# Ten columns of the input projection made for two token blocks from one weight load, in a hybrid decoder layer

## The chip, the cores and the metric

The kernel runs on one core of a Trainium2 chip. The metric is the device time of one execution in microseconds, lower is better. The engines are named as the profile names them: PE is TensorE (matmul) and PEld its loading of a weight matrix into the array, DVE is VectorE, ACT is ScalarE, POOL is GpSimd, SP is the engine whose queue issues the DMA transfers.

## The reference, cut to what matters

One layer of a decoder trunk over 2,048 prompt tokens and 32 sample tokens, width 1,024, in float32. A norm, one input projection to 2,560 columns (20 groups of 128, "columns" below), four mixers that each read a share of them, an output projection, a residual sum, a norm, a squared-ReLU MLP, a last norm:

```python
xn = rmsnorm(h, P['norm1_g'][l])
proj = xn @ P['w_in'][l]
p_ssm, p_q, p_f, p_i, p_g, p_rwkv, p_pool = jnp.split(proj, PROJ_SPLITS, axis=-1)
y_a, s_re, s_im = s5_mixer(p_ssm, ...)      # columns 0 and 1
y_b, s_hg = hgrn2_mixer(p_q, p_f, p_i, p_g, ...)   # columns 2 to 9
y_c, s_wkv, s_sh = rwkv7_mixer(p_rwkv, ...)  # columns 10 to 17
y_d, s_pool = pool_mixer(p_pool, ...)        # columns 18 and 19
mixed = jnp.concatenate([y_a, y_b, y_c, y_d], axis=-1).astype(h.dtype)
h = h + mixed @ P['w_out'][l]
h = h + sqrelu_mlp(rmsnorm(h, P['norm2_g'][l]), P['mlp_up'][l], P['mlp_down'][l])
```

The mixers are recurrent: each block of tokens needs the state that the block before it left.

## The kernel before, in words

The tokens lie along the free axis, in six blocks of 256, 384, 384, 384, 384 and 288 tokens (block 0 to block 5); features lie on the 128 partitions. Each matrix product is made in three matmuls on rounded parts: `mm24` runs 8 chunks of the contraction with three matmuls each (lines 157 to 159), 24 for one column of one block, each with its own load of 128 x 128 weights into the array.

A column's weights come as one transfer of 512 KB (`wload`, tile `raw`, two buffers), are rounded by ScalarE (`whi`, line 128) and subtracted by VectorE (`wlo`, line 129), three buffers each. `next_w` keeps one column split ahead, in the order of the list `wseq`, which `init_weights` writes: the columns of block 0 in order `IORD0`, those of block 1 in order `IORD1`, then output projection, MLP and later columns.

`inproj(b, part)` makes the columns of one block; `evac` takes a finished column out of PSUM (one of four tiles `mm`). Block 0 is not yet normalised there: its scale `y1` is multiplied in by VectorE in `evac`. Block 1 is normalised beforehand by `norm1(1)`: eight loads of x (line 204, two small buffers `xs`), the sum of squares (`sumsq`, lines 188 to 192), the scale (`rstd`, lines 168 to 178), then eight reloads of x, eight multiplications (line 216) and splits (lines 198 and 199) into `AB`, the operand of block 1's columns. Columns 0 to 9 of block 1 go to the tile `P10` (region `act1`), columns 10 to 17 to `P8` (region `h1`), columns 18 and 19 to the tile `pu`, which all blocks share. At the start `h1` holds block 0's x and then the scratch tile `su` of the SSM setup.

Beside the columns run generators that each yield after a step: `ssm_setup` (17 steps: constants of the SSM, mostly GpSimd, written to DRAM at the end), `lane1` (RWKV; 37 steps for block 0's two pairs of 128 tokens with their groupnorms), `lane2` (HGRN; 13 steps for each of block 0's two pairs), `l3` (SSM, 16 steps; needs the setup), and `lane4` (pooling, which reads `pu` and uses scratch that the setup leaves). `weave` advances each by a rate per step of the main generator; `drive` advances an interleaving of lanes 1, 2 and 3 by three steps per column. Then what is left of block 0's lanes is run out, with the next block's lanes taking turns as soon as one ends, and block 0's output projection begins; it reads all four mixers' results.

The order of this emission sets priorities: the framework's planner orders each engine's queue by it, and puts an instruction that it thinks ready ahead of earlier ones that are not. On the chip each engine then keeps the planned order. Tiles of one name reuse their buffers when the last reader is done.

Of the kernel before, what the change touches and what calls it, by code (L numbers as in the profile page):

```python
# [21 lines left out]
PM = 4  # L22
QA = lambda f: False
IORD = list(range(10)) + [18, 19] + list(range(10, 18))
IORD1 = list(range(20))
IORD0 = list(range(10, 18)) + list(range(2, 10)) + [18, 19, 0, 1]
CUT = 11
LAG = 2
HK = ()
# [1 line left out]
OK0 = (6, 7, 2, 3, 0, 1, 4, 5)  # L31
DEF = (0, 5)
WARM = 24
S1 = (1, 1, 0, 1, 8)
R1 = 3
S0 = (.6, 1, .06, 1, 3, 3, 3, .25, 1)
NG = {4: 1, 5: 1, 6: 9}


# [9 lines left out]
BLK = blocks()  # L49
# [3 lines left out]
class Main:  # L53
# [32 lines left out]
    def init_weights(self):  # L86
# [7 lines left out]
        outp = list(range(20, 28))  # L94
        seq += IORD0 + IORD1
        for b in range(nb):
# [125 lines left out]
    def scaled_parts(self, src, n, gcol, dst, square, ks=range(8)):  # L222

        nc = self.nc
        acc = None
        for k in ks:
            s = src(k)
            g = self.pp[:, gcol + k:gcol + k + 1]
            nc.scalar.activation(out=dst[:, k, :n], in_=s, func=AF.Copy, scale=g)
            nc.vector.scalar_tensor_tensor(out=dst[:, 8 + k, :n], in0=s, scalar=g, in1=dst[:, k, :n], op0=ALU.mult, op1=ALU.subtract)  # L230
            if square:
                acc = self.sumsq(lambda k: s, n, (k,), acc)
        return acc

    def norm1(self, b):
        return self.norm_to(lambda k: self.xload(b, k), BLK[b][2], 0, self.X(b))
# [143 lines left out]
def weave(main, *others, steps=None):  # L380

    acc = [0.0] * len(others)
    i = 0
    while i != steps:
        if next(main, END) is END:
            return
        i += 1
        for j, (g, rate) in enumerate(others):
            acc[j] += rate
            while acc[j] >= 1:  # L390
                acc[j] -= 1
                next(g, None)
# [64 lines left out]
def program(m):  # L457
    nb = len(BLK)
    if WARM:
        m.warm()  # L460
    run = lambda g: [None for _ in g]
    m.norm1_first()
    m.first_regions()
    m.l3 = m.lane3(0)
    main, setup, l1, l2, n1 = m.inproj(0, IORD0), m.ssm_setup(), m.lane1(0), m.lane2(0, False), m.norm1(1)
    weave(main, (setup, S0[0]), steps=8)
    weave(main, (l1, S0[1]), (setup, S0[2]), (n1, S0[7]), steps=8)
    weave(main, (l1, S0[1]), (setup, S0[2]), (l2, S0[3]), (n1, S0[8]))
    weave(n1, (l1, S0[4]), (setup, S0[5]), (l2, S0[6]))
    main = m.inproj(1, IORD1)  # L470
    weave(main, (l1, S1[0]), (l2, S1[1]), steps=S1[2])
    weave(main, (l1, S1[0]), (l2, S1[1]), (setup, S1[3]), steps=S1[4] - S1[2])
    run(setup)
    run(m.lane4())
    ready, done = [], []
    side = interleave(then(l1, done, ready, m.lane1(1)), then(l2, done, ready, m.lane2(1)), then(m.l3, done))
    drive(main, side, R1, rest=False)
    ready.append(1)
    while len(done) < 3:
        next(side)  # L480
    for b in range(nb):
        last = b + 1 == nb
        fin = m.final(b - 1) if last else None
        if last:
            next(fin)
        m.alloc_mlp(b)
        if last:
            run(lag_(m.outproj(b), fin, LAG))
            run(m.norm2(b))
        elif b:  # L490
            run(m.outproj(b))
            run(lag(m.inproj(b + 1, IORD[CUT:]), m.norm2(b), LAG))
        else:
            run(m.outproj(b))
            run(m.norm2(b))
        if b:
            side = None if last else m.mixers(b + 1)
        main = [m.mlp(b, m.norm1(b + 2) if b + 2 < nb else None)]
        if b + 2 < nb:
            main.append(lag(m.inproj(b + 2, IORD[:CUT], True), m.final(b), LAG * (2 if HK else 1)))  # L500
        elif last:
            main.append(m.final(b))
        drive(chain(*main), side, RATIO if b else R0)
        if b + 2 == nb:
            m.states_out()
# [101 lines left out]
class Mix(Main):  # L607
# [139 lines left out]
        nc.scalar.copy(self.sh[:, 1, i, :], v(ps[:, np_:n])[:, :, 3])  # L747

    def iord(self, b):
        return (IORD0, IORD1)[b] if b < 2 else IORD  # L750

    def region(self, b, k, tag, name):
        t = self.big.tile([128, k, NMAX], F32, tag=tag, name=name)
# [2 lines left out]
    def inproj(self, b, part, steps=False):  # L756
        n = BLK[b][2]
        X = self.X(b)
        held = []
        for c in part:  # L760
            if b and c == next(x for x in self.iord(b) if x < 10):
                self.P10[b % 2] = self.region(b, 10, f"act{b % 2}", "P10")
            if b and c == next(x for x in self.iord(b) if 10 <= x < 18):
                self.P8[b % 2] = self.region(b, 8, f"h{b % 2}", "P8")
            w = self.next_w(c)
            ps = self.psum()
            for _ in self.mmg(ps, w, lambda k: (X[:, k, :n], X[:, 8 + k, :n]), n):
                if steps:
                    yield
            held.append((c, ps))  # L770
            if b == 0 and c == part[0]:
                continue
            if b == 0 and c == part[1]:
                self.y1 = self.rstd(self.acc0, n)
            while held:
                self.evac(b, *held.pop(0))
            yield


    def rwkv_prep(self, b, c0, pool, par):  # L780
# [1256 lines left out]
```

## Time and profile before

| | |
|---|---|
| median of three runs | 2715.27 us (2713.78 to 2718.02) |
| the profiled execution's own time | 2714.48 us |
| its span, first to last instruction | 2712.6 us |
| TensorE busy / weight loads into the array | 97% / 92% |
| VectorE / ScalarE / GpSimd busy | 72% / 53% / 13% |
| mean granted TensorE clock | 0.982 of full speed |
| moved by DMA | 366.28 MB, 135 GB/s |

Busy shares are means over the span; a matmul's end is modelled, so a busy TensorE is not one at its peak. A granted clock of 1.00 is 2.4 GHz, 0.50 is 1.2 GHz; values between are means over a stretch that has both.

### The profile page before, as it was taken

What the parts mean: (1) busy time and instruction counts of PE and PEld (TensorE: products, weight loads), DVE (VectorE), ACT (ScalarE), POOL (GpSimd) and SP (SyncE); (2) the same over time, 40 slices, a digit from 0 to 9 for tenths busy, and PEclk for the clock granted to TensorE, in tenths of its full rate; (3) what the DMA queues carried; (4) which work ended last, traced back from release to release, by engine and by line L of the source; (5) the groups of instructions that cost most, each with busy time, mean ns of one, the idle gap of its engine ahead of it and who ended that gap; (6) DMA issues with size and microseconds to landing.
All of it is one profiled execution on the core that took longest, in us unless ns stands there. A gap on an engine that the chain in (4) does not pass through costs nothing.

```text
span 2712.6 us, 52883 instructions
## 1 busy us (share of the span) xinstructions
PE 2629.4 (97%) x20466; PEld 2492.0 (92%) x20466; DVE 1955.7 (72%) x4324; ACT 1438.6 (53%) x2377; POOL 357.5 (13%) x864
## 2 busy tenths in 40 slices
PE   8799899899999999999999999999999999999998
PEld 8688799889999999999999999999999989899997
DVE  7886888874877777487777748777775786557666
ACT  6544766544656545375654536565454754445443
POOL 7631201100111100001110010111001100000000
PEclk9799999999999999999999999999999999999999
DMA  6543344564333255532335553223555334435553
GB/s 208 142 126 98 124 148 134 156 190 147 115 96 98 96 166 165 166 119 88 99 101 174 167 160 113 94 91 107 173 177 159 100 103 122 133 115 169 167 168 127
DMA packets 221068, 366.28 MB, mean 135 GB/s; under 512 B 105520, under 2 KB 140912, under 8 KB 220816
## 3 DMA queue, kind: packets, MB, share of 16 engines
q1 hardware_dynamic: 220816, 362.90, 43.1%
q8 instruction: 161, 2.64, 0.4%
q14 instruction: 91, 0.75, 0.1%
HBM read 343.26 MB, written 17.99 MB: 133 GB/s over the span
## 4 chain that ended last, share of the span: by engine, by line
PE 74%; DVE 11%; DMA 5%; ACT 4%; POOL 3%; issue 2%; SPq 1%; DVEq 0%; ACTq 0%; POOLq 0%
PE mm L157 21%; PE mm L158 21%; PE mm L159 21%; DVE wlo L129 3%; DMA raw<-w 2%; PE x L1272 1%; ACT whi L128 1%; POOL XD L887 1%; POOL tm L885 1%; DMA xs<-xT 1%; PE x L687 1%; PE x L1828 1%; PE x L1827 1%; DMA mt<-dB 1%; PE x L951 1%
## 5 line engine op out<-in xcount | busy, mean ns | idle before, releaser
L128 ACT CAST whi<-raw 128x1024 fp32r<-128x1024 f32 x552 | 577.5, 1046 | 773.0 <-PE mm L158 528.0
L157 PE MATMUL mm<-AB,whi 128*128 128x384 f32 (+2 forms) x2880 | 950.4, 331 | 14.2 <-ACT whi L128 5.2
L159 PE MATMUL mm<-AB,wlo 128*128 128x384 f32 (+2 forms) x2880 | 936.2, 325 | 4.2 <-DVE wlo L129 3.8
L158 PE MATMUL mm<-AB,whi 128*128 128x384 f32 (+2 forms) x2880 | 935.2, 325 | 1.0 <-DVE AB L199 0.8
L129 DVE TENSOR_TENSOR wlo<-raw,whi 128x1024 fp32r<-128x1024 f32 x552 | 678.4, 1230 | 274.2 <-ACT whi L128 271.6
L157 PEld LDWEIGHTS mm<-AB,whi 128*128 128x128 f32 x2880 | 545.9, 190 | 27.3 <-ACT whi L128 6.3
L159 PEld LDWEIGHTS mm<-AB,wlo 128*128 128x128 f32 x2880 | 547.1, 190 | 9.3 <-DVE wlo L129 6.3
L158 PEld LDWEIGHTS mm<-AB,whi 128*128 128x128 f32 x2880 | 547.6, 190 | 6.7 <-DVE AB L199 1.4
L157 PE MATMUL mm<-act,whi 128*128 128x384 f32 (+2 forms) x1536 | 497.7, 329 | 4.6 <-ACT whi L128 2.5
L158 PE MATMUL mm<-act,whi 128*128 128x384 f32 (+2 forms) x1536 | 493.9, 323 | 0.5 <-DVE act L329 0.3
L159 PE MATMUL mm<-act,wlo 128*128 128x384 f32 (+2 forms) x1536 | 492.2, 322 | 0.0
L157 PEld LDWEIGHTS mm<-act,whi 128*128 128x128 f32 x1536 | 289.6, 190 | 12.9 <-DVE h L338 2.8
L158 PEld LDWEIGHTS mm<-act,whi 128*128 128x128 f32 x1536 | 291.2, 190 | 5.5 <-issue 2.3
L159 PEld LDWEIGHTS mm<-act,wlo 128*128 128x128 f32 x1536 | 290.6, 190 | 1.6 <-issue 0.2
L338 DVE TENSOR_TENSOR h<-h,mm 128x384 f32<-128x384 f32 (+2 forms) x384 | 192.5, 510 | 96.4 <-PE mm L159 95.6
L885 POOL TENSOR_TENSOR tm<-sq,XD 32x15 f32<-32x15 f32 (+7 forms) x240 | 90.7, 378 | 563.0 <-DMA sq<-XC 545.6
L329 DVE TENSOR_TENSOR act<-q,act 128x384 fp32r<-128x384 f32 (+2 forms) x192 | 98.9, 516 | 6.2 <-ACT q L326 1.7
L324 ACT ACTIVATE act<-r 128x384 fp32r<-128x384 f32 (+2 forms) x192 | 94.2, 490 | 13.3 <-DVE r L323 11.0
L887 POOL TENSOR_TENSOR XD<-XD,tm 32x15 f32<-32x15 f32 (+7 forms) x240 | 85.4, 356 | 18.5
L880 POOL MEMSET XD<- 32x512 f32 x16 | 8.3, 516 | 578.2 <-PE x L969 346.1
L192 DVE TENSOR_TENSOR acc<-acc,sq 128x384 f32<-128x384 f32 (+2 forms) x126 | 64.8, 514 | 15.7 <-ACT sq L191 13.3
L328 DVE TENSOR_TENSOR q<-r 128x384 f32<-128x384 f32 x128 | 71.1, 555 | 0.6 <-ACT r L321 0.5
(584 smaller groups left out, 3110.4 us busy)
## 6 DMA issues: line engine op xcount, KB each, us to landing
raw<-w SPq DMA_DIRECT2D x552, 512.0 KB
xs<-xT SPq DMA_DIRECT2D x96, 192.0 KB
yT<-xo SPq DMA_DIRECT2D x32, 192.0 KB
mt<-dB SPq DMA_DIRECT2D x20, 256.0 KB
mt<-dT SPq DMA_DIRECT2D x20, 256.0 KB
mt<-dC SPq DMA_DIRECT2D x20, 256.0 KB
xs<-xT SPq DMA_DIRECT2D x24, 144.0 KB
rt<-dRot SPq DMA_DIRECT2D x16, 98.0 KB
```

The costliest lines, as they stand in the source:

```text
L128: nc.scalar.copy(hi, raw)
L129: (nc.gpsimd if GW(i) else nc.vector).tensor_tensor(out=lo, in0=raw, in1=hi, op=ALU.subtract)
L157: nc.tensor.matmul(ps[:, :n], a, xh, start=k == ks[0], stop=False)
L158: nc.tensor.matmul(ps[:, :n], a, xl, start=False, stop=False)
L159: nc.tensor.matmul(ps[:, :n], c, xh, start=False, stop=k == ks[-1])
L192: nc.vector.tensor_tensor(out=acc[:, :n], in0=acc[:, :n], in1=q[:, :n], op=ALU.add)
L324: nc.scalar.activation(out=self.act[:, s, 0, :n], in_=r[:, :n], func=AF.Square)
L328: nc.vector.tensor_tensor(out=q[:, :n], in0=r[:, :n], in1=r[:, :n], op=ALU.mult)
L329: nc.vector.tensor_tensor(out=self.act[:, s, 1, :n], in0=q[:, :n], in1=self.act[:, s, 0, :n], op=ALU.subtract)
L338: nc.vector.tensor_tensor(out=self.h[:, d, :n], in0=self.h[:, d, :n], in1=ps[:, :n], op=ALU.add)
L885: g.tensor_tensor(out=w, in0=U[:, 0:t, t:t + 1].to_broadcast([32, t, m]), in1=XT[:, t:t + 1, t:16].to_broadcast([32, t, m]), op=ALU.mult)
L887: g.tensor_tensor(out=XT[:, 0:t, t:16], in0=XT[:, 0:t, t:16], in1=w, op=ALU.add)
```

## The change

Block 0 first makes its RWKV and pooling columns alone (10 to 19). Beside them block 1's norm is made by the new `norm1_second`: x is loaded once, into the region `act1`, and kept there for both passes. Then ten columns (2 to 9, 0 and 1) are made for both blocks, each from one transfer and one split of its weights (`inproj_both`). Then block 1 makes its own remaining ten, the pooling columns first. The rates at which the lanes and the setup advance are new: RWKV begins with the both-block columns (one step per block's column, 20 in all), HGRN with the last two of them (4 steps), and the setup makes 5 steps under the first ten columns, some 3 under the next ten, and the rest is emitted after them, followed by `lane4`. The stage with three lanes has 10 columns instead of 12.

```diff
-IORD1 = list(range(20))
-IORD0 = list(range(10, 18)) + list(range(2, 10)) + [18, 19, 0, 1]
+RWT = list(range(10, 18))
+BOTH = list(range(2, 10)) + [0, 1]
+IORD0 = RWT + [18, 19]
+IORD1 = BOTH + [18, 19] + RWT
...
-S1 = (1, 1, 0, 1, 8)
+S0 = (.5, 1.8)
+S1 = (1, .2, 1)
 R1 = 3
-S0 = (.6, 1, .06, 1, 3, 3, 3, .25, 1)
...
+    def norm1_second(self):
+
+        n = BLK[1][2]
+        x = self.region(1, 10, "act1", "x1")
+        acc = None
+        for k in range(8):
+            self.nc.sync.dma_start(out=x[:, k, :n], in_=self.D["xT"][128 * k:128 * k + 128, BLK[1][0]:BLK[1][0] + n])
+            acc = self.sumsq(lambda k: x[:, k, :n], n, (k,), acc)
+            yield
+        yield from self.norm_to(lambda k: x[:, k, :n], n, 0, self.X(1), acc)
...
-    main, setup, l1, l2, n1 = m.inproj(0, IORD0), m.ssm_setup(), m.lane1(0), m.lane2(0, False), m.norm1(1)
-    weave(main, (setup, S0[0]), steps=8)
-    weave(main, (l1, S0[1]), (setup, S0[2]), (n1, S0[7]), steps=8)
-    weave(main, (l1, S0[1]), (setup, S0[2]), (l2, S0[3]), (n1, S0[8]))
-    weave(n1, (l1, S0[4]), (setup, S0[5]), (l2, S0[6]))
-    main = m.inproj(1, IORD1)
-    weave(main, (l1, S1[0]), (l2, S1[1]), steps=S1[2])
-    weave(main, (l1, S1[0]), (l2, S1[1]), (setup, S1[3]), steps=S1[4] - S1[2])
+    main, setup, l1, l2, n1 = m.inproj(0, IORD0), m.ssm_setup(), m.lane1(0), m.lane2(0, False), m.norm1_second()
+    weave(main, (setup, S0[0]), steps=2)
+    weave(main, (setup, S0[0]), (n1, S0[1]))
+    run(n1)
+    main = m.inproj_both(BOTH)
+    weave(main, (l1, S1[0]), (setup, S1[1]), steps=16)
+    weave(main, (l1, S1[0]), (l2, S1[2]), (setup, S1[1]))
     run(setup)
     run(m.lane4())
     ready, done = [], []
+    main = m.inproj(1, [18, 19] + RWT)
...
+    def inproj_both(self, part):
+
+        for c in part:
+            w = self.next_w(c)
+            if c == part[0]:
+                self.P10[1] = self.region(1, 10, "act1", "P10")
+            for b in range(2):
+                X, n = self.X(b), BLK[b][2]
+                ps = self.psum()
+                self.mm24(ps, w, lambda k: (X[:, k, :n], X[:, 8 + k, :n]), n)
+                self.evac(b, c, ps)
+                yield
```

## Rows read from the trace of the kernel before

**Rows 1.** Windows, from 300 us to the end; columns as in rows 3.
```profile
300.00:2712.60 2412.60, 2366.58 (x18291) 2251.28 (x18291) 1726.62 (x3768) 1273.92 (x2092) 223.69 (x534) 0.99 0.43 134
```

**Rows 2.** Timeline of PE at 79 us; bracketed: idle before, releaser.
```profile
79.10 0.47 PE L1272 MATMUL x<-P,E 64*64 64x64 f32 x2 [8.51 <-ACT E L1209]
```

**Rows 3.** Windows: stretch, length, busy PE, PEld, DVE, ACT, POOL, PEclk, DMA, GB/s.
```profile
8.40:49.20 40.80, 34.46 (x247) 32.29 (x245) 27.96 (x64) 23.66 (x38) 30.46 (x92) 0.92 0.64 198
96.80:110.40 13.60, 6.21 (x60) 4.72 (x58) 13.56 (x34) 6.26 (x12) 5.20 (x8) 0.65 0.88 221
110.40:129.10 18.70, 17.91 (x88) 15.69 (x87) 17.52 (x39) 8.67 (x19) 11.67 (x26) 0.71 0.50 134
129.10:187.50 58.40, 55.75 (x527) 50.55 (x526) 46.14 (x111) 32.16 (x54) 25.53 (x51) 0.94 0.43 116
187.50:255.20 67.70, 66.14 (x643) 62.31 (x642) 45.65 (x143) 25.24 (x43) 11.76 (x35) 0.97 0.44 126
255.20:281.00 25.80, 20.03 (x133) 17.13 (x133) 18.45 (x41) 19.49 (x36) 9.02 (x14) 0.88 0.08 27
```

**Rows 4.** Timelines of PE and DVE: the norm of block 1.
```profile
69.68 0.81 PE L168 MATMUL nrm<-acc,ones 128*128 128x384 f32 x2
...
105.78 0.54 DVE L178 TENSOR_TENSOR ny<-ny,nt 128x384 f32<-128x384 f32 x1
...
126.47 1.08 DVE L199 TENSOR_TENSOR AB<-xn,AB 128x384 fp32r<-128x384 f32 x1
```

**Rows 5.** Timeline of PE (start us, length us): matmuls 18, 18, 12 apart.
```profile
94.10 0.28 PE L157 MATMUL mm<-AB,whi 128*128 128x256 f32 x1
96.23 0.28 PE L157 MATMUL mm<-AB,whi 128*128 128x256 f32 x1
...
229.53 0.34 PE L157 MATMUL mm<-AB,whi 128*128 128x384 f32 x1
232.69 0.34 PE L157 MATMUL mm<-AB,whi 128*128 128x384 f32 x1
...
79.89 0.41 PE L157 MATMUL mm<-AB,whi 128*128 128x256 f32 x1
82.45 0.41 PE L157 MATMUL mm<-AB,whi 128*128 128x256 f32 x1
```

**Rows 6.** Lines, first 260 us (count | busy us, mean ns | idle before).
```profile
L129 DVE TENSOR_TENSOR wlo<-raw,whi 128x1024 fp32r<-128x1024 f32 x43 | 53.9, 1255 | 21.0 <-ACT whi L128 20.8
L216 DVE SCALAR_TENSOR_TENSOR xn<-xs,pp_sb,ny 128x384 f32<-128x384 f32 x8 | 6.9, 878 | 0.8 <-DMA xs<-xT 0.7
L199 DVE TENSOR_TENSOR AB<-xn,AB 128x384 fp32r<-128x384 f32 x8 | 4.9, 631 | 0.1
L192 DVE TENSOR_TENSOR acc<-acc,sq 128x384 f32<-128x384 f32 x7 | 3.9, 550 | 1.1 <-ACT sq L191 1.1
```

**Rows 7.** Timelines of PE and SP: the setup's closing matmuls, last transfers.
```profile
151.58 0.57 PE L1727 MATMUL mm<-su 128*16 128x128 f32 x2
...
181.48 3.65 SPq L1731 DMA_DIRECT2D dT<-su  x8
```

**Rows 8.** Lines, 160 to 266 us: HGRN operations of the second pair.
```profile
L1287 DVE COPY_PREDICATED P<-cst,x 128x32 f32<-128x32 int32 x24 | 2.7, 195 | 0.0
L1413 ACT ACT_TABLE_LOAD x2 | 2.6, 1283 | 2.2 <-DVE E L1412 2.2
L1272 PE MATMUL x<-QK 64*64 64x32 f32 x96 | 2.5, 220 | 0.0
L1415 DVE TENSOR_TENSOR eb<-eb,E 128x256 f32<-128x256 f32 x2 | 0.9, 426 | 2.8 <-ACT E L1414 2.8
```

**Rows 9.** Timeline of all engines: the tail.
```profile
256.11 0.68 PE L987 MATMUL x<-sv,M 128*64 128x64 f32 x8
...
277.32 0.42 DVE L1185 TENSOR_TENSOR AB<-Y,AB 128x256 fp32r<-128x256 f32 x1
...
281.91 0.36 PE L157 MATMUL mm<-AB,whi 128*128 128x256 f32 x1
```

More of the change, by code (lines that the diff above doesn't have):

```diff
@@ L749, in iord @@
     def iord(self, b):
-        return (IORD0, IORD1)[b] if b < 2 else IORD
+        return IORD1 if b < 2 else IORD
     def region(self, b, k, tag, name):
```

## The prediction

> **What bounds the kernel now.** I cut the span into stages with the table of windows, at the ends of columns as the timeline of TensorE shows them. From 300 us on TensorE is busy 2366.6 of 2412.6 us at a granted clock of 0.99 [rows 1]: there is little left to win there, nothing after it is edited, and whatever is won or lost before 300 us is carried to the end almost unchanged. Only time in which TensorE stands still or runs slowly counts. So the whole question lies in the first 281 us: 20 columns for the first block (to 96.8 us), 20 for the second (110.4 to 255.2), with the first block's mixers in between, and a tail to 281 in which the output projection waits for the last mixer results.
>
> In the first 281 us the reader is to see three losses. At 70.6 us TensorE stops for 8.51 us in the middle of a column, because a matmul of the HGRN lane stands ahead of the column's others in its queue and waits for ScalarE [rows 2]. From 96.8 to 110.4 no column runs; VectorE is busy 13.56 of 13.60 us there [rows 3]. The reason is the second block's norm: its sum of squares left TensorE at 69.68 us, the scale was ready at 106.3 and the last normalised part at 127.6 [rows 4], each step standing in VectorE's full queue. Then the first two columns of the second block take 18.7 us, part of it at half clock (0.71 in that window).
>
> What a column costs when nothing waits: 18 of its 24 matmuls are 2.13 us apart at 256 tokens, so 2.85 for 24; 3.16 us at 384 tokens, so 4.21; and at half clock 12 take 2.56 us, so 5.1 a column of 256 tokens [rows 5].
>
> **The change, part by part.** It removes ten loads of 512 KB, ten ScalarE casts and ten VectorE subtractions of 1.26 us [rows 6]. It does not remove one matmul or one array weight load: each block still runs 24 of each per column. So on TensorE it saves nothing directly; the ten subtractions are 12.6 us of an engine that is full only in the two stages from 96.8 to 129.1 (31.1 of 32.3 us) [rows 3]. What counts is the new order, and I add it up as a clock, stage by stage.
>
> *Stage 1, ten columns of block 0 with the norm beside them.* Before, the tenth column ends at 49.2 us, and VectorE worked 27.96 of the 40.8 us [rows 3]. The norm adds 3.9 + 6.9 + 4.9 us [rows 6] and five short operations of about 0.5 [rows 4], near 18 us: 46 us of work, over 40.8. It cannot be hidden wholly. Its eight loads of x (192 KB) are no longer held back by two small buffers, and eight reloads vanish, since x stays in the free `act1` region; but the loads go out in SP's queue among the first weights, while DMA already works at 0.64 [rows 3]. If VectorE were always busy the norm would be done at 54.4, at 90% at 59.5. The columns need only their own small evacuations, so I take 52 for the tenth column (49.2 to 57), and 4 us (0 to 10, the latter being 18.7 minus two columns in today's wait) lost before the second block's columns run freely: 56.
>
> *Stage 2, ten columns for both blocks.* 10 x (2.85 + 4.21) = 70.6 us, with 20 steps of the RWKV lane, 4 of HGRN and some 4 of the SSM setup between them. Today's 187.5 to 255.2 holds ten columns (42.1) and 30 lane steps, so 25.6 us or 0.85 a step; 129.1 to 187.5 holds eight columns (33.7) and 24 steps, so 1.03 a step [rows 3]. 28 steps are 24 to 29; I take 24, since VectorE has its load halved here (one subtraction per 7 us). The stage ends at 56 + 70.6 + 24 = 150.6. Today the same thirty column pieces are done at 187.5.
>
> *Handover.* Here the new order costs. Columns 18 and 19 of block 1 come first in the next stage, but their target `pu` is still being read by block 0's pooling, which waits for the rest of the setup (now all emitted after the both-block columns); and the RWKV columns write the region `h1`, which the setup holds until its last copies to DRAM. Today the setup's last transfers go out at 181.5 to 185.1, after its first closing matmuls at 151.6 [rows 7]; the pooling is done earlier, and nothing waits, since the first RWKV column of block 1 starts only at 187.5. In the new order that is 33.5 us counted from 150.6, so to 184. Four PSUM tiles let four columns go ahead of their evacuation, 4 x (4.21 + 2.56, the lane steps of a column) = 27 us: 6.5 left, or 13 if one of the four is in use by the setup or the SSM lane, or nothing if the planner draws the setup's work forward. I take 5.
>
> *Stage 3, ten columns of block 1 with 30 lane steps:* today's 67.7 us for the same count [rows 3]. End: 150.6 + 5 + 67.7 = 223.3, against 255.2 today.
>
> *The tail.* HGRN has 26 steps for block 0. Today 14 are emitted before the three-lane stage and 12 in it: none is left when the columns end, only 3 of RWKV. In the new order HGRN starts 4 steps before that stage and makes 10 in it; 12 steps, nearly all of its second pair, are left with no column to hide them, beside 7 of RWKV and 4 of SSM. The pair's own durations one after another, from the table of lines [rows 8]: the masks 2.7, the level matmuls 2.5 and as many again for their other part and the state, two table loads 2.6, and some 45 further operations, most near 0.43 and some below 0.3, about 18: 28 us, the lower bound. It does not have its engines alone: in today's tail VectorE is busy 18.45 and ScalarE 19.49 of 25.8 us [rows 3], largely for the other lanes. With its engines two thirds of the time the chain takes 42, which I take (28 to 74, the latter below): 265.3.
>
> *After it* three output columns, of which only the pooling quarter can be done in advance: 3 x 2.85 x 0.75 = 6.4, partly at half clock: 7. The fourth would start at 272.3; today it starts at 281.9 [rows 9]. That is 9.6 us sooner. The profiled execution took 2714.48 us (span 2712.6), 0.8 below the median of the runs: 2714.5 - 9.6 + 0.8 = 2705.7.
>
> On that tail the rows say that after stretches with few matmuls the granted clock is low (0.65 and 0.71 in the two windows after 96.8, 0.88 in today's tail) [rows 3]. The Trainium skill, "TensorE: Matmul & The Clock Gate", Part 1, states the rule behind it: the throttled clock is the default and activity releases it. By the rule the longer tail would leave all three output columns at half clock, 3 x 5.1 x 0.75 = 11.5 instead of 7, and the sum would be 2710; by today's tail, where only some of their matmuls are slow, it is 2706. The same page (Part 2) says that matmuls stay in program order, which is what the 8.51 us wait shows and what can happen anew wherever a lane's matmul is placed too early.
>
> **The rivals.**
> *The tail eats more than was won (slower).* Place: from the last column of block 1 to the last write of HGRN's second pair. Today's tail runs the last 3.5 RWKV steps from 256.11 to 277.74, 21.6 us [rows 9], 6.2 a step; twelve at that rate are 74 us, 32 more than I took: +22, 2738 us. It decides from a tail of 51.6 us (4.3 a step) on. For it: three lanes interleave there, each engine takes them in the planner's order, and the clock is low. Against it: groupnorm's steps, which fill today's tail, are longer than most of HGRN's.
> *The handover and the norm eat it (same).* The upper bound of 13 instead of 5 and 2 us more in stage 1: 2716, within 0.2% of before (5.4 us, about what a measurement can tell from no change). For it: two regions and the PSUM tiles are shared. Against: the setup's VectorE and GpSimd work is ready early, and GpSimd is busy only 25.5 of the 58.4 us from 129.1 on [rows 3].
> *The tail is hidden (faster still).* If the pair runs at its own durations, 28: 14 us less, 2692. For it: VectorE is busy only 45.65 of today's 67.7 us of stage 3 [rows 3], so the pair's first steps could run ahead. Against: in today's tail each step takes far longer than its own operations.
> *That the change does nothing* is excluded: 542 weight casts in place of 552, and the order differs from the first microseconds on.
>
> **How the numbers follow.** My forecast, 2698 to 2709, has 0.45; the hidden tail 0.12; the handover case 0.20; the long tail 0.23. Faster by over 0.2%: 0.57; within: 0.20; slower: 0.23. The range runs from just under the hidden tail, 2690, into the long one, 2728 (that is, a tail of 64 us).
>
> **What would show it.** Right: 542 casts; no column-free stretch like 96.8 to 110.4; the second block's norm done by about 60 us; the thirtieth column piece at about 151, the last column of block 1 at about 223, the fourth output column at about 272, and an unchanged course after it. Wrong: in stage 1, if the tenth column ends after 57; at the handover, if columns stand for more than 13 us behind `pu` or `h1`; in the tail, if it lasts over 51 us; or if the time after 300 us changes by more than 2 us, which no term here explains.

## The result, and the profile after

The changed kernel takes 2749.33 us (2747.84 to 2752.75, 4 runs) beside 2714.53 for the kernel before on the same chip: ratio 1.0115, 95% interval 1.0102 to 1.0129. It is slower by 35 us; 2706 was forecast, with a range up to 2728. The profiled span is 2746.7 us against 2712.6. One of the executions of run e1 below is left out of its numbers: it took 3173.92 us at a granted clock of 0.743.

The same stages as in [rows 3], cut at the ends of columns. Windows of the changed kernel: stretch, length, busy PE, PEld, DVE, ACT, POOL, PEclk, DMA share, GB/s:

```profile
8.05:60.11 52.06, 37.69 (x257) 34.27 (x256) 34.81 (x78) 32.72 (x54) 38.38 (x118) 0.90 0.63 199
60.11:103.92 43.81, 34.12 (x223) 33.32 (x222) 32.45 (x60) 17.97 (x35) 28.44 (x70) 0.88 0.24 70
103.92:160.90 56.98, 54.78 (x457) 51.41 (x455) 33.71 (x76) 24.56 (x44) 18.88 (x41) 1.00 0.31 88
160.90:188.49 27.59, 12.96 (x98) 8.74 (x97) 23.01 (x48) 10.88 (x20) 17.93 (x41) 0.70 0.41 101
188.49:251.63 63.14, 63.14 (x581) 59.25 (x582) 37.86 (x124) 26.16 (x42) 11.44 (x33) 0.97 0.43 127
251.63:304.33 52.70, 37.63 (x392) 31.98 (x393) 36.51 (x118) 28.54 (x56) 8.34 (x16) 0.71 0.12 25
345.19:358.73 13.54, 5.00 (x76) 3.97 (x76) 11.83 (x36) 7.62 (x16) 0.00 (x0) 0.63 0.29 95
622.00:2746.00 2124.00, 2093.41 (x15544) 1993.81 (x15544) 1489.42 (x3184) 1099.54 (x1788) 183.42 (x429) 1.00 0.42 133
```

The reader is to see two stretches in which TensorE does little at a low granted clock while VectorE is busy: 160.90 to 188.49, where no column runs (VectorE 23.0 of 27.6 us), and 345.19 to 358.73 (11.8 of 13.5). In a table, against the clock that the prediction set up:

| point | forecast | measured | before |
|---|---|---|---|
| tenth column of block 0 ends | 52 | 60.1 | 49.2 |
| thirtieth column piece ends | 150.6 | 160.9 | 185.5 |
| time without columns after it | 5 | 27.6 | 2.1 |
| last column of block 1 ends | 223.3 | 251.6 | 255.2 |
| last mixer result written | 265.3 | 294.6 | 277.3 |
| fourth output column starts | 272.3 | 304.3 | 281.9 |

Up to there the forecast is 32.0 us out: 10.3 in the first two stages, 22.6 in the handover, 4.6 back in stage 3, 1.0 in the tail (43.0 for 42) and 2.7 in the output columns. Behind that point "an unchanged course" was forecast. It did not come. The offset of a column below is its start minus that of the same column in the kernel before, columns counted from the last one backwards: +22.4 us at the fourth output column, +24.3 at the first up column (before: 301.1 us), +39.3 at the first down column (324.2), +31.6 at 622 us and at 666, +33.9 at the last column.

Block 1's norm, forecast for about 60, has its scale at 61.3 us and its last part at 87.4. The largest wait of stage 1 stands before its tenth column: a lane's matmul waits for ScalarE, then the norm's first matmul for VectorE, and the column comes behind both. Timeline of PE (start us, length us; bracketed: idle before, releaser):

```profile
50.95 0.37 PE L825 MATMUL x<-tha,wl 64*128 64x128 f32 x1 [1.37 <-ACT tha L819]
...
54.06 1.65 PE L170 MATMUL nrm<-acc,ones 128*128 128x384 f32 x2 [2.39 <-DVE acc L194]
54.94 0.99 PE L159 MATMUL mm<-AB,whi 128*128 128x256 f32 x1
```

The handover, timeline of PE:

```profile
174.69 3.59 PE L1753 MATMUL mm<-su 128*16 128x128 f32 x16
187.53 1.03 PE L1753 MATMUL mm<-su 128*16 128x128 f32 x4 [9.25 <-DVE su L1743]
188.49 0.69 PE L159 MATMUL mm<-AB,whi 128*128 128x384 f32 x1
```

The setup's first group of closing matmuls (line 1727 of the kernel before) and four of the second come first and the columns behind them; the second group waits for VectorE's line 1743. After 345 us it is the scale of block 0's second norm that is late (lines 174 to 180; line 336 is the first evacuation of an up column, which needs it). Timeline of DVE, only some of the operations in between:

```profile
337.38 0.42 DVE L174 TENSOR_SCALAR acc<-nrm 128x256 f32<-128x256 f32 x1
343.56 0.43 DVE L177 TENSOR_TENSOR nt<-ny 128x256 f32<-128x256 f32 x1 [2.02 <-ACT ny L176]
...
345.29 0.42 DVE L1232 SCALAR_TENSOR_TENSOR lf<-P,L 128x256 f32<-128x256 f32 x1 [0.97 <-ACT L L1230]
...
347.66 0.42 DVE L178 TENSOR_TENSOR nt<-nt,acc 128x256 f32<-128x256 f32 x1
...
349.58 0.29 DVE L179 TENSOR_SCALAR nt<-nt 128x256 f32<-128x256 f32 x1
349.79 1.22 DVE L131 TENSOR_TENSOR wlo<-raw,whi 128x1024 fp32r<-128x1024 f32 x1
350.92 1.10 DVE L1270 TENSOR_TENSOR QK<-bb 128x128 f32<-128x128 f32 x5
...
353.71 0.42 DVE L180 TENSOR_TENSOR ny<-ny,nt 128x256 f32<-128x256 f32 x1
...
357.52 0.43 DVE L336 SCALAR_TENSOR_TENSOR r<-mm,ny 128x256 f32<-128x256 f32 x1
```

Five operations that need 2 us on VectorE take 16.7 from first to last. The way over ScalarE behind the first of them takes 5.8 us, hardly more than in the kernel before (5.3); the last four take 10.6 where there it is 1.7, since block 1's HGRN (lines 1232 and 1270) and weight splits stand between them. Four up columns fill the four PSUM tiles meanwhile; the fifth starts at 358.73, 1.2 us after the first evacuation began. In the kernel before the same chain has nothing between its last four steps and ends in 7.4 us:

```profile
313.25 0.42 DVE L172 TENSOR_SCALAR acc<-nrm 128x256 f32<-128x256 f32 x1 [1.59 <-PE nrm L168]
318.98 0.42 DVE L175 TENSOR_TENSOR nt<-ny 128x256 f32<-128x256 f32 x1 [2.02 <-ACT ny L174]
...
320.22 0.45 DVE L178 TENSOR_TENSOR ny<-ny,nt 128x256 f32<-128x256 f32 x1
```

### The profile page after: what moved, and what is told of

It is laid out like the page before. It is cut to its first block, busy times and chain, and to the rows that moved or that the text cites. A ratio compares the mean times of both kernels' runs of the same rounds, so it can differ in the third digit from the quotient of the medians.

```text
span 2746.7 us, 52803 instructions
## 1 busy us (share of the span) xinstructions
PE 2633.7 (96%) x20466; PEld 2494.7 (91%) x20466; DVE 1947.0 (71%) x4314; ACT 1433.2 (52%) x2369; POOL 356.9 (13%) x864
## 4 chain that ended last, share of the span: by engine, by line
PE 70%; DVE 10%; POOL 5%; DMA 5%; ACT 4%; issue 3%; SPq 2%; DVEq 0%; ACTq 0%; POOLq 0%
PE mm L159 20%; PE mm L161 20%; PE mm L160 20%; DVE wlo L131 2%; DMA raw<-w 2%; POOL XD L913 2%; POOL tm L911 2%; PE x L1298 1%; ACT whi L130 1%; PE x L700 1%; PE x L1853 1%; PE x L1854 1%; DMA xs<-xT 1%; DMA yT<-xo 1%; PE x L995 1%
## 5 line engine op out<-in xcount | busy, mean ns | idle before, releaser
L130 ACT CAST whi<-raw 128x1024 fp32r<-128x1024 f32 x542 | 566.5, 1046 | 772.0 <-PE mm L160 551.0
L131 DVE TENSOR_TENSOR wlo<-raw,whi 128x1024 fp32r<-128x1024 f32 x542 | 665.4, 1228 | 279.3 <-ACT whi L130 270.9
L911 POOL TENSOR_TENSOR tm<-sq,XD 32x15 f32<-32x15 f32 (+7 forms) x240 | 98.6, 411 | 532.5 <-DMA sq<-XC 515.4
L194 DVE TENSOR_TENSOR acc<-acc,sq 128x384 f32<-128x384 f32 (+2 forms) x126 | 65.9, 523 | 11.8 <-ACT sq L193 9.2
```

The source lines that it names most:

```text
L130: nc.scalar.copy(hi, raw)
L131: (nc.gpsimd if GW(i) else nc.vector).tensor_tensor(out=lo, in0=raw, in1=hi, op=ALU.subtract)
L194: nc.vector.tensor_tensor(out=acc[:, :n], in0=acc[:, :n], in1=q[:, :n], op=ALU.add)
L911: g.tensor_tensor(out=w, in0=U[:, 0:t, t:t + 1].to_broadcast([32, t, m]), in1=XT[:, t:t + 1, t:16].to_broadcast([32, t, m]), op=ALU.mult)
```

## The experiments

All results in one table; the text takes them in turn. "u" is the offset of the first up column, "d" that of the first down column, "m" that at 666 us, the second block's last output column. Offsets come from one profiled execution each. In the thirteen other runs whose first stage is emitted as in the change the tenth column ends at 57.1 to 59.5 us (60.1 in the change), so differences of up to 3 us between offsets say little.

| run | us | ratio to before | u | d | m |
|---|---|---|---|---|---|
| the change | 2749.3 | 1.0115 (1.0102 to 1.0129) | +24.3 | +39.3 | +31.6 |
| e1 setup early | 2743.0 | 1.0092 (1.0071 to 1.0114) | +16.6 | +28.8 | +22.6 |
| e2 setup's PSUM | 2749.6 | 1.0110 (1.0094 to 1.0125) | +22.9 | +37.6 | +30.7 |
| e3 lanes held | 2743.9 | 1.0091 (1.0074 to 1.0107) | +22.1 | +30.3 | +27.7 |
| e4 norm only | 2741.9 | 1.0079 (1.0063 to 1.0096) | +20.0 | +25.8 | +22.3 |
| e5 norm, steps kept | 2722.8 | 1.0021 (1.0012 to 1.0030) | +3.1 | +3.9 | +0.8 |
| e6 HGRN ahead | 2744.5 | 1.0103 (1.0082 to 1.0125) | +25.5 | +32.1 | +26.9 |
| e7 setup and lanes | 2728.0 | 1.0035 (1.0016 to 1.0055) | +3.5 | +9.8 | +9.5 |
| e8 lanes held, 5 | 2768.6 | 1.0185 (1.0168 to 1.0202) | +23.0 | +31.9 | +49.6 |
| e9 e7, lanes held | 2732.6 | 1.0054 (1.0038 to 1.0070) | +3.1 | +10.0 | +18.5 |
| e10 two loads | 2746.6 | 1.0110 (1.0089 to 1.0131) | +28.1 | +37.8 | +28.7 |
| e11 lanes held, 17 | 2786.1 | 1.0251 (1.0228 to 1.0275) | +20.8 | +29.0 | +66.7 |
| e12 no norm | 2738.8 | 1.0082 (1.0062 to 1.0102) | +17.0 | +31.5 | +19.8 |
| e13 no second scale | 2741.0 | 1.0089 (1.0072 to 1.0106) | +24.2 | +19.8 | +20.9 |
| e14 e7, no second scale | 2721.0 | 1.0021 (1.0011 to 1.0032) | -0.3 | -2.1 | -0.4 |
| e15 scale on GpSimd | 2743.2 | 1.0090 (1.0076 to 1.0104) | +23.9 | +29.7 | +26.3 |
| e16 e7, scale on GpSimd | 2730.6 | 1.0043 (1.0029 to 1.0057) | +2.6 | +4.6 | +12.8 |
| e17 before, setup ops moved | 2715.6 | 0.9990 (0.9980 to 0.9999) | -2.5 | -2.3 | 0.0 |
| e18 e7, setup ops moved | 2725.4 | 1.0025 (1.0014 to 1.0036) | -3.7 | +3.5 | +5.2 |

**e1, the setup earlier.** The setup's rate beside the both-block columns, and two steps of the SSM lane that it carries put behind those columns:

```diff
-S1 = (1, .2, 1)
+S1 = (1, .65, 1)
-    run(setup)
+    next(m.l3), next(m.l3), run(setup)
```

> The changed kernel with the SSM setup emitted faster beside the both-block columns (rate .65 in place of .2), so that its closing steps no longer stand between those columns and the second block's own. Theory (the closing steps, emitted last, hold the columns): the 27.6 us without columns shrink to under 6, and the time falls by 17 to 22 us to 2727-2732. Rival (the closing steps cost their engine time wherever they are): the both-block columns, 101 us long, grow by about what the gap loses, and the time stays within 5 us of 2749.

Windows from the last both-block column on:

```profile
169.56:171.69 2.13, 2.13 (x19) 1.72 (x19) 1.83 (x4) 1.51 (x4) 0.00 (x0) 1.00 0.27 40
171.69:237.11 65.42, 65.42 (x638) 60.80 (x638) 41.80 (x135) 28.05 (x47) 12.13 (x35) 1.00 0.44 127
237.11:299.65 62.54, 42.45 (x399) 36.11 (x399) 42.61 (x131) 34.06 (x65) 9.77 (x16) 0.67 0.13 30
```

The 27.6 us shrink to 2.1: late setup steps do stop the columns. The price is another matter. The both-block stage ends 8.7 us later (169.6), the last column 14.5 us sooner, and the stretch from it to the fourth output column is 62.5 us instead of 52.7: of 25.5 us taken out, 4.7 are left at that column. Both theories were partly right, neither in its number.

**e2, the setup's PSUM tiles.** Both kinds of closing matmuls:

```diff
-                pt = self.psum().rearrange("p (a n) -> p a n", a=4)
+                pt = self.px().rearrange("p (a n) -> p a n", a=4)
-                pg = self.psum()
+                pg = self.px()
```

> The changed kernel, but the setup's transposes and closing matmuls write the lanes' PSUM tiles and not the four of the columns. If the four PSUM tiles are what holds the second block's own columns behind the setup, the pooling columns 18 and 19 run ahead of the setup's last matmuls: 8 us (two columns of 4.2) come off the gap of 27.6, and 2741 is to be seen. If the regions pu and h1, or VectorE and GpSimd, hold them, the gap stays above 25 us and the time within 3 us of 2749.

Columns 18 and 19 now do run ahead (161.9 to 173.7), and then the stop is back, 27.73 us; the last column ends 2.5 us sooner, and nothing is left of it in the time. Columns put into the gap bring nothing: they were not what the first block's end waits for.

**e3, block 1's lanes held** until block 0's have ended:

```diff
-    ready.append(1)
     while len(done) < 3:
         next(side)
+    ready.append(1)
```

> The changed kernel, but the second block's lanes may not begin before all three of the first block's have ended. After the tail the changed kernel lost another 12 us beside the up columns. Theory (the second block's lane matmuls, emitted during the long tail, stand in TensorE's queue ahead of the up columns and wait): the stop of 13.5 us at 345 us goes, 2737-2740. Rival (the second norm's own chain is late behind the crowded VectorE and ScalarE): the first down column stays 36-39 us later than in the kernel before, and the time stays within 4 us of 2749 or rises, since lane work is lost from the tail.

The stop before the fifth up column falls from 13.5 to 9.4 us only, the chain of the scale to 15.5. Neither forecast hit; e8, e11, e13 and e15 go on with it.

**e4 and e5, the norm alone** in the kernel before, at 1.8 steps a column from the third on; e5 (last two lines) also keeps what the norm's last step carried:

```diff
-    main, setup, l1, l2, n1 = m.inproj(0, IORD0), ..., m.norm1(1)
+    main, setup, l1, l2, n1 = m.inproj(0, IORD0), ..., m.norm1_second()
...
-    weave(n1, (l1, S0[4]), (setup, S0[5]), (l2, S0[6]))
+    weave(iter([0]), (l1, S0[4]), (setup, S0[5]), (l2, S0[6]))
```

> The kernel before with one part of the change alone: the second block's norm made beside the first block's columns from x kept in the act1 region; no shared columns, no other order. If that norm was what made the 13.6 us without columns and the two slow columns after them (18.7 us for two, 8.4 when nothing waits), 10 to 20 us come off: 2695-2705. Rival (VectorE is the limit there and the norm's 18 us only move): the first twenty columns end later by what the stretch loses, and the time stays within 5 us of 2714.

> The norm alone once more, in the kernel before, but with the three steps each of RWKV, setup and HGRN put back that were carried by the norm's last step and were lost in the run before this one. Theory (the lost steps made that run slow: the setup's closing steps then stopped the columns for 17 us): that stop falls below 6 us and the kernel comes out 5 to 15 us under the kernel before, 2700-2710. Rival (the norm beside the first block's columns is itself the loss): it stays over 2730.

e4 lost 22 us, with a stop of 17.0 us at 162.6 us; three steps more of RWKV, of HGRN and of the setup take it away (3.3 us at that place). The stop stands where the rest of the setup is emitted: five steps in e4, two in e5. So a few steps of emission decide over 22 us at 666, some 16 by the ratios. Neither forecast of e5's time was hit, and without that loss the early norm is worth nothing (+0.8 us at 666, ratio 1.0021): the 13.6 us without columns [rows 3] go, but the first twenty columns end at 112.4 instead of 96.8. VectorE works 81.1 us up to there, against 64.7 in the kernel before up to 96.8: the norm moved, with its cost.

**e6, HGRN ahead, and e7, both** (e7 with e1's second edit too, and RWKV a little faster):

```diff
-S1 = (1, .2, 1)
-R1 = 3
+S1 = (1, .2, 3)        # e6
+S1 = (1.2, .65, 3)     # e7
+R1 = 4
```

> The changed kernel with HGRN's lane emitted faster: three steps for each of the last four both-block pieces instead of one, and four lane steps per own column of the second block instead of three. The setup is left as it is. Theory (the chain of the mixers, HGRN's above all, sets the end of the tail, since its work begins at 200 us and not at 79): the 44 us from the last column to the end of the first output column fall under 30, and 2725-2737 is to be seen. Rival (the lanes' engines are full, so that the steps only move): the ten own columns, 63 us long, grow by what the tail loses, and the time stays within 5 us of 2749.

> Both remedies in the changed kernel: the setup at rate .65 beside the both-block columns, and RWKV at 1.2, HGRN at 3 and four lane steps per column. If the late setup and the late lanes are together what the change lost, the fourth output column starts before 285 us and 2700-2720 is to be seen. If each only moves its cost to the next stage, the fourth output column stays near 300 us and the time over 2735.

Windows of e6, then of e7: the time without columns, the ten own columns, the stretch to the fourth output column:

```profile
162.86:203.14 40.28, 13.92 (x124) 9.57 (x124) 33.85 (x76) 21.31 (x38) 24.98 (x52) 0.61 0.27 69
203.14:270.21 67.07, 66.32 (x647) 61.70 (x646) 35.59 (x122) 19.83 (x33) 6.95 (x23) 0.98 0.46 128
270.21:304.39 34.18, 22.32 (x153) 18.22 (x153) 23.22 (x56) 22.40 (x44) 8.60 (x15) 0.85 0.05 17
```

```profile
176.53:182.25 5.72, 5.72 (x89) 4.36 (x88) 5.40 (x26) 4.10 (x10) 1.13 (x5) 1.00 0.41 86
182.25:257.33 75.08, 71.53 (x677) 65.87 (x678) 49.90 (x166) 35.58 (x61) 11.17 (x36) 0.95 0.40 112
257.33:285.96 28.63, 16.54 (x113) 15.09 (x113) 19.89 (x47) 21.77 (x41) 7.38 (x10) 0.76 0.07 21
```

In e6 the last stretch falls from 52.7 to 34.2 us as its theory has it, but HGRN's steps now stand ahead of the setup's, and the time without columns grows from 27.6 to 40.3: the fourth output column starts at 304.4, where it was, and the time misses the forecast (2744.5). Alone, e1 brought 4.7 us there and e6 none; together they bring 18.4 (285.96; 285 and at most 2720 us were expected). The three runs fit one reading: the first block's mixers and the setup are one body of dependent work that must be done before the output projection, and columns only fill it. How late HGRN's was, one line of each trace shows (the level matmuls; first to last start), of the kernel before, the change and e7:

```profile
L1272 PE MATMUL x<-QK x1536: 192/219/313, 92.1 to 2251.4; 64*64 64x32 f32 x192
```

```profile
L1298 PE MATMUL x<-QK x1536: 192/219/313, 202.1 to 2287.0; 64*64 64x32 f32 x192
```

```profile
L1298 PE MATMUL x<-QK x1536: 189/219/242, 161.3 to 2265.9; 64*64 64x32 f32 x192
```

**e10, the shared load undone,** the order kept:

```diff
-        seq += IORD0 + IORD1
+        seq += IORD0 + [c for c in BOTH for _ in range(2)] + [18, 19] + RWT
...
-            w = self.next_w(c)
             for b in range(2):
+                w = self.next_w(c)
```

> The changed kernel's order kept whole, but the shared load undone: each of the ten columns is loaded, cast and subtracted once for each block, 552 casts as in the kernel before. If the ten casts and the 12.6 us of subtractions saved count in the both-block stage (101 us, VectorE about two thirds busy), the stage grows by 5 to 12 us and 2754-2762 is to be seen. If the one load is worth nothing that the path sees, the time stays within 4 us of 2749.

The stage grows by 4.2 us (165.1), the stop to 30.1, and the rest of the way takes it back (m +28.7): the one load is worth nothing in the time.

**e8, e11 and e9, block 1's lanes held longer:** e3 and these lines (17 for 5 in e11); e9 is e7 with e8's edits.

```diff
-        drive(chain(*main), side, RATIO if b else R0)
+        main = chain(*main)
+        if b == 0:
+            [next(main) for _ in range(5)]
+        drive(main, side, RATIO if b else R0)
```

> The changed kernel with the second block's lanes held until the first block's are done, and also until the five first up columns and the scale of the second norm are emitted. Holding them in the tail alone left a stop of 9.4 us before the fifth up column and the scale's chain at 15.5 us (7.4 in the kernel before). Theory (the second block's lane operations stand between the steps of that scale on VectorE and ScalarE, and the four PSUM tiles are full until it is there): the chain falls to 8 us or less, the stop to under 3, and the time to 2733-2738. Rival (the lane work is only put off and comes back as a wait later): the stop goes and the time stays at 2741-2746.

> The changed kernel with the second block's lanes held until the first block's are done and until the first up columns and twelve steps after them are emitted: longer than in the earlier run with five, in which the planner still drew lane operations of the second block between the steps of the second norm's scale (chain 15 us, stop 9.3 us before the fifth up column). Theory (those operations stretch the chain): the chain falls under 9 us and the stop under 3 us; the time is above 2755 all the same, since the lane work comes back as a wait at 600 us. Rival (the chain is slow for another reason, such as the two table loads): the stop stays at 9 us or more.

> The run with the faster setup and lanes (1.0035 of the kernel before), with the second block's lanes held as in the run before this one. If what was left of the loss is the stop of 6.8 us before the first down column, the ratio comes to 0.999-1.002. If the lane work put off comes back later, it stays at 1.003-1.005.

Both forecasts failed in e8 and the theory's in e11: the stop stays at 9.3 and 9.4 us. But the edit didn't do what it was for: HGRN's operations of block 1 still stand between the scale's steps, drawn forward in the planned order, so these two runs tell nothing of the stop. They show something else. Windows from 600 to 700 us of the kernel before, e8 and e11:

```profile
600.00:700.00 100.00, 97.42 (x532) 95.45 (x532) 54.86 (x87) 46.06 (x67) 9.75 (x10) 0.97 0.47 146
```

```profile
600.00:700.00 100.00, 84.58 (x514) 76.48 (x513) 45.99 (x99) 33.54 (x50) 1.50 (x7) 0.85 0.44 127
```

```profile
600.00:700.00 100.00, 76.15 (x592) 68.62 (x590) 45.66 (x124) 30.22 (x48) 6.87 (x20) 0.80 0.36 102
```

The second block's mixers, put off, stop TensorE there. In e9 too the lane work put off comes back: as late as e7 at the first down column, it is 9 us later at 666. A lead did not last either where nothing is held: e14 is 4.8 us ahead at 612 us and level at 653, while e17's 2.3 us are gone by 361. What takes them was not tried.

**e12, the first norm left out** in `norm1_second`:

```diff
-            acc = self.sumsq(lambda k: x[:, k, :n], n, (k,), acc)
...
-        yield from self.norm_to(lambda k: x[:, k, :n], n, 0, self.X(1), acc)
+        for k in range(8):
+            self.split(self.X(1), k, x[:, k, :n], n)
```

> The changed kernel without the sum of squares, the scale and the multiplications of the second block's norm: x is loaded and split as it is, so some 13 us of VectorE work and the wait for the scale are left out of the first 100 us. The both-block stage began 4 us later and ended 10 us later than forecast. If the columns set the end of the first block, those 10 us come off: 2737-2740. If the mixers' lanes set it, the both-block columns end 10 us or more sooner and the time falls by less than 5: 2744-2749.

The both-block stage ends 6.9 us sooner (154.0), m falls by 11.8, the time by some 9 in ratio: nearer to the first theory. It is an upper bound for that norm, since its VectorE time goes too and the lanes gain by it.

**e13 and e14, the second scale left out** for block 0, in the change and in e7:

```diff
-                self.y2 = self.rstd(self.y2, n)
+                self.y2 = self.np.tile([128, NMAX], F32, tag="ny", name="ny", bufs=2)
+                nc.vector.memset(self.y2[:, :n], 1.0)
```

> The changed kernel with the scale of the first block's second norm left out (ones in its place), so that the up columns' evacuations wait for no chain on VectorE and ScalarE. Theory (that chain, stretched to 16 us by the second block's lane operations between its steps, fills the four PSUM tiles and stops TensorE for 13.5 us): the stop falls under 4 us and the time to 2735-2740. Rival (the second block's lane matmuls in TensorE's own queue are what stops it): the stop stays above 9 us, 2745-2750.

> The run with the faster setup and lanes (ratio 1.0035), with the same scale left out. There the stop before the first down column was 6.8 us. If the chain is what is left of the loss after 300 us, the ratio comes to 1.000-1.002, what the later fourth output column (4 us) is worth; if the lane matmuls are, it stays at 1.003-1.005.

Both leave out work that the kernel before does, so they bound what the scale's chain costs and are no remedies. The stop is gone in e13: the fifth up column starts at 340.5, the first down column at 344.0 (363.5 in the change). So the scale is what TensorE waited for, not the lane matmuls. Of 19.5 us there, 10.7 are left at 666. In e14 the whole loss is gone at 666; what is left of its ratio lies behind 1734 us in the profiled execution (offset -0.2 there, +3.3 at the last column; that execution is the fastest of its ten).

**e15 and e16, the scale's last four steps on GpSimd** (lines 177 to 180, for block 0's second norm alone), in the change and in e7:

```diff
-        nc.vector.tensor_tensor(out=t[:, :n], in0=y[:, :n], in1=y[:, :n], op=ALU.mult)
+        nc.gpsimd.tensor_tensor(out=t[:, :n], in0=y[:, :n], in1=y[:, :n], op=ALU.mult)
...
```

> The changed kernel whole, with the last four operations of the first block's second scale moved from VectorE to GpSimd, which is busy 16 of 100 us there. Theory (the second block's lane operations between those steps on VectorE stretch the chain to 16 us): the chain falls to 9-12 us, the stop of 13.5 us to under 8, and 5 us or more come off: 2739-2745. Rival (the two steps on ScalarE with their table loads are what is slow): the chain stays over 14 us and the time within 3 us of 2749.

> The run with the faster setup and lanes (ratio 1.0035), with the same four operations on GpSimd. Leaving the scale out took it to 1.0021, level with the kernel before until 1700 us. If moving its steps does half of that, the stop of 6.8 us falls to 3 and the ratio comes to 1.001-1.003; a ratio under 1 is expected by neither theory.

Timeline of POOL in e15:

```profile
341.74 0.61 POOL L178 TENSOR_TENSOR nt<-ny 128x256 f32<-128x256 f32 x1 [12.78 <-ACT ny L176]
342.43 0.72 POOL L179 TENSOR_TENSOR nt<-nt,acc 128x256 f32<-128x256 f32 x1
343.24 0.41 POOL L180 TENSOR_SCALAR nt<-nt 128x256 f32<-128x256 f32 x1
343.72 0.77 POOL L181 TENSOR_TENSOR ny<-ny,nt 128x256 f32<-128x256 f32 x1
```

Each step is slower there, and the chain shorter: 9.0 us from its first step at 335.5 in place of 16.7. The stop falls to 7.5 us and m by 5.3: VectorE's queue was what stretched it, as the theory says. e6 shows the same without moving a step: nothing stands between the last four there (346.64 to 348.30 us), the chain takes 6.6 us and the fifth up column does not wait, though the fourth output column is as late as in the change; the way from the first up to the first down column is still 6.6 us longer than in the kernel before. In e16 the first stop halves (6.8 to 3.6), but the first down column then takes 12.7 us (3.0 in e7), and the ratio is no better than e7's.

**e17 and e18, two setup operations moved.** VectorE stands idle at the same spot in the kernel before and in the change. Timelines of DVE, of the one and of the other:

```profile
74.56 1.70 DVE L1603 TENSOR_TENSOR P<-P 128x128 f32<-128x128 f32 x1 [6.79 <-POOL P L1598]
```

```profile
66.55 1.14 DVE L218 SCALAR_TENSOR_TENSOR xn<-x,pp_sb,ny 128x384 f32<-128x384 f32 x2
75.69 1.70 DVE L1629 TENSOR_TENSOR P<-P 128x128 f32<-128x128 f32 x1 [8.01 <-POOL P L1624]
...
77.66 0.60 DVE L218 SCALAR_TENSOR_TENSOR xn<-x,pp_sb,ny 128x384 f32<-128x384 f32 x1
```

One setup operation waits for GpSimd, and behind it in the queue the lanes' operations and, in the change, the second block's norm. The edit, in `cmul`, moves that operation and the next to GpSimd, for the kernel before (e17) and for e7 (e18):

```diff
-            big = vtt if n > 100 else tt
+            big = tt
```

> The kernel before with two setup operations (the sum and difference of one complex product, 128 x 128) moved from VectorE to GpSimd, which makes their inputs. In every trace so far VectorE stands 6 to 8 us near 68-76 us for GpSimd at the first of them, with the norm and the lanes queued behind it. Theory (that one wait makes the column of 14.8 us at 69 us, and the similar one in the changed kernel): the wait goes, that column falls under 9 us, and 4 to 7 us come off, ratio 0.9975-0.9985. Rival (the work behind it has slack): the columns after it end at the same time and the ratio stays within 0.999-1.001.

> The run with the faster setup and lanes (ratio 1.0035), with the same two operations moved to GpSimd. The norm of the second block waits behind them in VectorE's queue at 68 us, and the second both-block column took 16 us. Theory: the both-block stage ends 6 to 8 us sooner, ratio 1.0005-1.002. Rival (the lanes set the end): the stage ends sooner and the fourth output column does not, ratio 1.003-1.004. Under 1 is reached only if it gains more than here the kernel before gains.

The wait went, and the next setup operation took one like it; of e17:

```profile
83.79 0.75 DVE L1687 TENSOR_TENSOR su<-P 128x256 f32<-128x256 f32 x1 [8.30 <-DMA dRot<-su]
```

The column of 14.8 us takes 3.4, and two columns later TensorE stops for 8.8. 2.5 us are left at 301 us and none at 666. In e18 the both-block stage ends only 1.5 us sooner than in e7 (175.0; 6 to 8 were expected); it gains 4.3 us over e7 at 666 and stays slower than the kernel before. No version with the shared columns was faster than the kernel before; e17's 0.999 is the only ratio under 1, and is within the 0.2% of no change.

## Why the prediction was wrong, step by step

**The step that failed first** is "Handover ... I take 5" with its bound of 13: 27.6 us. "Four PSUM tiles let four columns go ahead" was read off the number of tiles, not off the queue: no column ran ahead of the setup's closing matmuls. With those on other tiles two columns did (e2), so the tiles were part of it; what held the columns after these two (the regions, or the planned order) was not tried apart. That the setup's late steps make the stop is shown by e1: by the code ten of its 17 steps are emitted behind the both-block columns in the change (four, not five, stand under the first ten columns), and one in e1. In another kernel e4 against e5 agrees, though steps of two lanes differ there too.

**The step that failed most** is the form of the sum. It added stages of TensorE's clock, and priced what was moved out of a stage as time won. e1 and e6 took 25.5 and 18.5 us out of one stage and saw 20.8 and all of it come back in others. What the runs show in its place is that the first block's mixers and the setup together set its end, and the change starts HGRN's level matmuls 110 us later (202 for 92). Both together made early again (e7) bring back 18 of the 22 us at the fourth output column, 22 of 31.6 at 666.

**Stages 1 and 2** were 10.3 us out, 8.1 of it in stage 1, which ended past its bound of 57. "The columns need only their own small evacuations" failed: the norm's first matmul stood ahead of the tenth column and waited for VectorE. With the norm left out (e12) that column ends at 55.8 and stage 2 ends 6.9 us sooner, an upper bound for the norm's part. Stage 2 took 2.2 us more than its price (100.8 for 98.6), in part by luck: VectorE was not "always busy" in it but stands 8.0 us for GpSimd with the norm queued behind, a wait that no term holds. The reading of the stop at 79 us in the kernel before [rows 2] as a lane matmul placed too early stopped one step short: the lane was late because VectorE stood 6.8 us for GpSimd just before; with that wait moved (e17) TensorE's stop moved too.

**The tail**: 42 forecast, 43.0 measured. Its mechanism was right: HGRN's second pair runs behind the last column (level matmuls up to 274.6 us). That the size fits is in part luck, since it moves with the other stages: in e1 the stretch from the last column to the fourth output column is 62.5 us for 52.7. The rival that the tail would eat the gain was not what happened. The granted clock was 0.71 in that stretch, and the output columns at its end took 9.7 us, between the 7 taken and the 11.5 of half clock throughout.

**"An unchanged course after it"** (within 2 us) failed by the 13.5 us stop, some of which came back by 622 us: 7.3 us are left between the first up column and 666. The scale as its cause is shown (e13), VectorE's queue as what stretches it too (e15). Why block 1's operations are ready just then in the change and not in the kernel before was not settled; in e6, as late, none stands there, so lateness alone does not do it.

**The removed work** was rightly priced at nothing on the whole: 542 casts, and no time from the ten loads (e10), whose 4.2 us in their own stage came back behind it. That the early norm wins time was wrong: alone it wins none (e5).

## What to carry to other kernels

Before stages are added up on one engine's clock, ask what sets the end of the phase: if it is a chain on other engines, time taken out of one stage returns in the next, and an order is judged by when that chain's first links start. An operation that waits on another engine holds everything behind it in its queue, so follow a stall from the engine that shows it back to the queue in which it began. And run one part of a change alone with the emission of all else kept: e4 and e5 differ by nine steps and, by their ratios, by some 16 us.

## What the runs showed of the hardware that was not expected

A slower engine with a free queue beat a faster one with a full queue: the scale's steps took 0.41 to 0.77 us on GpSimd and 0.29 to 0.43 on VectorE, and the chain was 7.7 us shorter. The Trainium skill, "GPSIMD Engine Reference", in its opening, calls GpSimd the wrong choice for ordinary elementwise arithmetic, VectorE being about twice as fast. The durations come near that (1.4 to 1.8 times); as advice it did not hold for this chain.

After the 27.6 us with few matmuls (granted clock 0.70) the first column of the second block alone took 8.2 us, later ones 4.5. Its first twelve matmuls took 3.9 us, where twelve at the later pace take 2.1: some 1.8 us are the clock's, at its lower level (1.2 GHz), and the rest went to fourteen matmuls of the setup and of pooling within the column.

e5 and e14 were level with the kernel before until 1734 us (+0.7 and -0.2) and behind at the last column (+6.5 and +3.3). So was e17 (-1.4 and +3.1), whose ratio is under 1: one profiled execution does not tell what the last 1,000 us hold, and it was not tried.
